# 1/rms rows through DRAM, a hand-ordered start and moved places in a hybrid decoder step

## The chip, the cores and the metric

The kernel runs on one core of one Trainium2 chip, as one launch. The metric is the device time of that launch in microseconds, the median of several runs. A profile of one execution is read beside it; it has its own time, which is named below.

The engines are called as in the profile: PE is the matrix engine (PEld its weight loads), DVE the vector engine, ACT the scalar engine, POOL the GpSimd engine, SP the engine that only issues DMAs here.

## The reference

One decoder layer. 2048 prompt tokens (zero initial state) and 8 decode rows (with given states) of width 1024 go through an RMS norm, one projection to eight groups of 512 columns, two chunkwise recurrences with four heads each, a norm by head, gates, an output projection, a residual and a final RMS norm. Cut to what matters:

```python
def mixer_layer(x, pos, s_ret, s_hg, norm_g, w_in, ret_g, hg_g, lb, w_out):
    h = rmsnorm(x, norm_g)
    p = (h @ w_in).astype(jnp.float32)
    rq, rk, rv, rg, hq, hf, hi, hgate = jnp.split(p, 8, axis=-1)
    rq = rotary(rq.reshape(B, L, RET_HEADS, RET_DK), pos)
    rk = rotary(rk.reshape(B, L, RET_HEADS, RET_DK), pos) * (RET_DK ** -0.5)
    ...
    o_ret, s_ret_new = chunked_decay_recurrence(rq, rk, rv, log_gamma, s_ret)
    o_ret = head_rmsnorm(o_ret, ret_g) * jax.nn.silu(rg)
    logf = jnp.logaddexp(jnp.log(lbf), jnp.log1p(-lbf) + jax.nn.log_sigmoid(hf))
    kin = (1.0 - lbf) * jax.nn.sigmoid(-hf)
    ...
    o_hg, s_hg_new = chunked_decay_recurrence(silu(hq), kin, hi, logf, s_hg)
    o_hg = head_rmsnorm(o_hg, hg_g) * jax.nn.silu(hgate)
    y = x + jnp.concatenate([o_ret, o_hg], axis=-1) @ w_out
```

Everything is fp32 in and out. The outputs are the two y, and the four new states.

## The kernel before

**Products.** Every large matrix product is done by Strassen's scheme on 2 x 2 blocks (seven products for eight, in the Winograd form, with block sums S1 to S4 of one side and T1 to T4 of the other), and each operand is split into a high and a low part of fp32r, so that a product of one 128-deep slice is three matmuls (high by high, high by low, low by high). One of the seven products is four slices, so 12 matmuls of 128 x 512. `product` (L872) issues half of one, 6 matmuls.

**Units and places.** The main loop has 38 units of seven products, numbered -6 to 31. A place is a number: unit u holds the places 7u to 7u + 7, and the seven products of a unit stand at 0, 1, 3, 4, 5, 6 and 9 behind 7u (`SLOTS`), so that one place is about one product. Units -6 to -1 make the values (columns rv and hi) of one pair of 128-token chunks each; 0 to 23 make the other six groups, three units for a head and half of the tokens (H: HGRN2 f and q, G: the gates, R: retention k and q); 24 to 31 are the output projection. All other work (splits, sums, gates, the recurrences, the decode rows, loads) is put on a list as `at(place, function)`, and at the end the list is emitted in order of place. `after(d, f)` puts f at d places behind the current one. The table `AT` holds most of the places.

**Queues.** Each engine works through its own instructions in the order in which they were emitted; this holds for PE in the whole kernel (`manual_schedule`), for DVE, ACT, POOL and SP from the second pair's ordered block on (`ORDERED`). Ahead of that block, in the start, the order of these four is left to the tile framework's own scheduler. A DMA on SP or POOL waits in its queue for its buffer or its source, and what is behind it waits too.

**The norm.** For each pair, `stats_load` and `stats_sum` (L332) square the token rows on ACT and `root` (L336, L228, L229) makes 1/rms on POOL: one value per partition (token), in `rs_all`. The transposed tokens (`x_t`) have the tokens along the free dimension, so 1/rms is needed as a row on all partitions. `spread_dg` (L356) makes a diagonal matrix of it on DVE, `spread` (L363) multiplies it on PE by a matrix of ones, and `tok_norm` (L372) on DVE multiplies tokens, gain `g_in` and this row from PSUM. `x1_dg` (L1316) and `x1_spread` (L701, L702) do the same for the second half of the tokens, and store two rows blocks to `rb_dram`, which `x1_rb` loads eight times later. `decode_dg` (L579) and `decode_spread` (L583, L585, L586) do it for the eight decode rows.

**The start.** After warm-up matmuls on constants (`wu`, L200, L203) pair 0 and then pair 1 are multiplied plainly, 96 matmuls each (`plain_k`, L465), while the W_v weights are loaded, split (`wv_split`, L233) and their differences T1 to T4 made (`wv_subs`, L514) and split (`wv_parts`, L233). Then the eight W_v slices are multiplied with the decode rows (`decode_values`, L556), for which `decode_inputs` (L532) multiplies them by the gain. Half of the differences of the slices 2 and 3 are made and split in the loop (`wv_late`).

**Blocks for later.** `blocks_sums` (L434) makes the differences T1 to T4 of the tokens of four pairs, half of them on POOL; POOL stores them (L430), SP loads them when they are needed (L1465).

**The recurrences.** `ret_rec` and `hgrn_rec` have steps with places of their own behind 7u (`AT["ret"]`, `AT["hgrn"]`): scores (s; s0 to s3, in which DVE updates k and q, L1188, L1191, and PE makes small score products, L1223, L1275, L1284), the value load, k transposed (k), the chunk updates (u), the states (st0, st1, DVE L1069), the outputs (o0, o1, L1076, L1078), and after scaling on ACT the transposition back and the gate (t0, t1, DVE L1103).

Of the kernel before, what the change touches and what calls it, by code (L numbers as in the profile page):

```python
# [15 lines left out]
ALU = mybir.AluOpType  # L16
# [32 lines left out]
def spooled(u):  # L49
# [10 lines left out]
          'load': 18.0,  # L60
# [10 lines left out]
 'ret': {'load': 12.0,  # L71
# [16 lines left out]
       'sS1': -1.4,  # L88
# [3 lines left out]
       'sA12': 1.4,  # L92
       'sS3': 2.4,
       'sA22': 3.05},
 're': {'A11': -3.4, 'S1': -2.4, 'S2': -1.4, 'S4': -0.4, 'A12': 0.6, 'S3': 1.6, 'A22': 2.6},
 'dec': {'mm': -1.97, 'mm0': -3.42, 'copy': -0.9, 'copy0': -2.4, 'sel': 0.7},
# [10 lines left out]
          'B22': (8.9, 8.95, 9.2, 9.75),  # L107
          'B21': (9.45, 9.85, 10.0, 10.3),
          'T3': (11.3, 11.3, 11.8, 11.8),
          'T4': (14.2, 14.2, 14.7, 14.7)},  # L110
# [4 lines left out]
           'lB21': 6.4,  # L115
           'lT3': 8.4,
           'lT4': 12.2,
           'B11': (3.0, 3.0, 3.5, 3.5),
# [3 lines left out]
           'B21': (9.45, 9.85, 10.0, 10.3),  # L122
# [6 lines left out]
 'wu': 17,  # L129
 'wop': (140.0, 1.8, 2.0, 2.6),  # L130
 'gate': {'G': 0.7, 'store': 1.2, 'R': 0.8, 'H': 0.7, 'root': 0.5, 'scale': 1.0, 'gt': 1.2, 'tr': 0.6},
 'fin': 0.75,
# [11 lines left out]
 'dhs': (-5.0, -2.2, -2.2, -1.5)}  # L144
# [5 lines left out]
def step_kernel(ctx, tc, a, out):  # L150
# [22 lines left out]
    vd_dram = dr.tile([2, NB, GW], F32, tag="vd_dram", name="vd_dram")  # L173
    v_dram = [
# [151 lines left out]
    def stats_sum(i, ahead=False):  # L326
# [23 lines left out]
    dgs = {}  # L350

    def spread_dg(i):
        dgs[i] = []
        for c in (2 * V_ORDER[i], 2 * V_ORDER[i] + 1):
            dg = vq.tile([P, P], F32, tag="dg", name=f"dg{c}", bufs=2)
            dve.tensor_scalar(dg, ident, rs_all[:, c : c + 1], None, op0=ALU.mult)  # L356
            dgs[i].append(dg)

    def spread(i):
        p = V_ORDER[i]  # L360
        pt = ps_tr.tile([P, 2, P], F32, tag="tr", name=f"prs{p}")
        for j, dg in enumerate(dgs[i]):
            pe.matmul(pt[:, j], ones, dg, start=True, stop=True)  # L363
        spread_to[i] = pt.rearrange("p a b -> p (a b)")
# [59 lines left out]
    def blocks_sums(i, n):  # L424
# [8 lines left out]
        def less(o, x, y):  # L433
            (dve if (i, n) in ((6, 0), (7, 1)) else pool).tensor_tensor(o, x, y, op=ALU.subtract)  # L434
# [35 lines left out]
    def tok_load0(i, k0, cuts=1):  # L470
        r = x0r[i, k0] = t_get([P, 2, 256], f"x0r{i}{k0}")
        for n in range(0, 2, 2 // cuts):
            kk = slice(n, n + 2 // cuts)
            sp.dma_start(r[:, kk], a["x_t"][V_ORDER[i], :, k0 + kk.start : k0 + kk.stop])
# [101 lines left out]
    dgd = vq.tile([NB, NB], F32, tag="dgd", name="dgd")  # L576

    def decode_dg():
        dve.tensor_scalar(dgd, ident[:NB, :NB], rsd[:, 1:2], None, op0=ALU.mult)  # L579

    def decode_spread():
        pt = ps_tr.tile([P, NB], F32, tag="tr", name="prsd")
        pe.matmul(pt, ones[:NB, :], dgd, start=True, stop=True)  # L583
        rb = vq.tile([P, NB], F32, tag="rbd", name="rbd")
        act.activation(rb, pt, AF.Copy)  # L585
        dve.tensor_tensor(  # L586
            xz[:, : 32 * KT].rearrange("p (k b) -> p k b", b=32)[:, :, :NB], xs,
            rb.unsqueeze(1).to_broadcast([P, KT, NB]), op=ALU.mult,
        )
# [11 lines left out]
    tok_load0(0, 0, 2)  # L601
    wv_load(0, 2)
    act.activation(lb[:, 0:1], zero, AF.Sigmoid)
    tok_load0(0, 4)
    wv_load(4, 2)
    for k in (0, 4):
        x_split0(0, k)
        wv_split(k)
    wv_load(1)
    wv_load(5)  # L610
    for k in (1, 5):
        x_split0(0, k)
        wv_split(k)
    tok_load0(0, 2)
# [12 lines left out]
    sp.dma_start(pk, a["pack"])  # L627
    stats(1)
    decode_inputs()
    for k in range(KT):  # L630
        x_split0(1, k)
    pv0 = {(c, ty): bank([P, GW], f"pv0{c}{ty}") for c in range(2) for ty in range(2)}
# [5 lines left out]
    for m, k in enumerate((0, 4, 1, 5, 2, 6, 3, 7)):  # L638
        decode_values(m, k)
    first, second = ("T1", "T2"), ("T3", "T4")  # L640
# [9 lines left out]
    with tc.manual_schedule(engines=ORDERED):  # L650
        stats_load(2)
        for c in range(2):
            for ty in range(2):
                plain_out(0, c, ty, pv0[c, ty])
        wv_subs(0, first + second)
        wv_parts(0, first + second)
        tok_load(2)
        ps = plain_next(0, 1)
        stats_sum(2, True)
        stats_load(3)  # L660
        wv_subs(1, first + second)
        wv_parts(1, first + second)
        tok_load(3)
        plain_out(1, 0, 1, ps)
        stats_sum(3, True)
        spread_dg(2)
        ps = plain_next(1, 1, lambda: spread(2))
# [3 lines left out]
        wv_subs(2, first[:1])  # L671
        wv_subs(3, first[:1])
# [4 lines left out]
        wv_parts(2, first[:1])  # L677
        wv_parts(3, first[:1])
        tok_norm(2, 1)
        tok_sums(2, 0)  # L680
        s_split(2, "S1")
        plain_out(1, 0, 0, ps)
        wv_subs(2, second[:1])
        wv_subs(3, second[:1])
        wv_subs(2, first[1:])
        wv_subs(3, first[1:])
        wv_parts(2, first[1:])
        wv_parts(3, first[1:])
        s_split(2, "S2")
        tok_sums(2, 1)  # L690
        s_split(2, "S4")
        ps = plain_next(1, 0)
# [5 lines left out]
    def blk_spread(blk, dg, dst):  # L698
        pt = ps_tr.tile([P, 4, P], F32, tag="tr", name=f"prb{blk}")
        for j in range(4):  # L700
            pe.matmul(pt[:, j], ones, dg[:, j], start=True, stop=True)  # L701
        act.activation(dst, pt.rearrange("p a b -> p (a b)"), AF.Copy)  # L702

# [1213 lines left out]
```

## Time and profile before

| | |
|---|---|
| median of 3 runs | 1004.38 us (1004.34 to 1006.59) |
| the profiled execution's own time | 1006.96 us |
| its span, first to last instruction | 1005.2 us |
| busy PE / DVE / ACT / POOL | 987.3 / 783.6 / 574.6 / 256.2 us |
| granted clock of PE, mean | 0.998 |
| moved by DMA | 244.56 MB, 243 GB/s |

How to read it: busy time is the time in which an engine had an instruction running; a wait row says which engine waited for whom, in total, how many times and the longest. The chain of waits is followed back from the last instruction, at each step to what released it. A fence shows rows as the profile has them; a line number is that of the kernel before. Between the last instruction and the execution's own time lie 1.8 us that the span doesn't hold.

### The profile page before, as it was taken

How to read it: one execution, taken by the hardware profiler on the slowest of the kernel's cores; microseconds unless marked ns; L12 is line 12 of the kernel's file. 1: busy time of each engine (PE TensorE's matmuls, PEld its weight loads, DVE VectorE, ACT ScalarE, POOL GpSimd, SP SyncE). 2: the span in 40 equal slices, each digit the busy share in tenths (PEclk: the TensorE clock that was granted, in tenths of full speed). 3: DMA queues.
4: the chain of work that ended last, by engine and by line, in shares of the span. 5: the costliest groups of instructions: out<-in, count | busy, mean ns of one | idle time of the engine just before them, and what ended most of it. 6: DMA issues, size and time to landing. Idle time of an engine off the chain costs nothing.

```text
span 1005.2 us, 22979 instructions
## 1 busy us (share of the span) xinstructions
PE 987.3 (98%) x8824; PEld 822.0 (82%) x8824; DVE 783.6 (78%) x1361; ACT 574.6 (57%) x1348; POOL 256.2 (25%) x404
## 2 busy tenths in 40 slices
PE   9999999999999999999999999999999999999997
PEld 8788877888888888888788788888888878877885
DVE  6797696879869978887898766877866799767774
ACT  7754523847655664765885555456467577524332
POOL 0211271112332433232012222222222602313121
PEclk9999999999999999999999999999999999999999
DMA  9746659838958878785985993993996396674522
GB/s 332 242 150 238 222 189 357 313 114 298 305 171 306 304 239 287 279 253 184 348 261 175 303 321 119 304 335 109 309 370 218 111 406 228 238 263 155 206 88 83
DMA packets 121340, 244.56 MB, mean 243 GB/s; under 512 B 12128, under 2 KB 52448, under 8 KB 118544
## 3 DMA queue, kind: packets, MB, share of 16 engines
q1 hardware_dynamic: 97968, 164.68, 48.9%
q0 software_dynamic: 22976, 78.17, 21.0%
q8 instruction: 69, 1.13, 0.5%
q14 instruction: 39, 0.32, 0.1%
q10 hardware_dynamic: 288, 0.27, 0.1%
HBM read 155.97 MB, written 90.24 MB: 245 GB/s over the span
## 4 chain that ended last, share of the span: by engine, by line
PE 84%; DVE 7%; ACT 4%; issue 2%; DMA 1%; POOL 1%; POOLq 0%; SPq 0%; DVEq 0%; ACTq 0%
PE aH L872 9%; PE aG L872 8%; PE aO L872 7%; PE aR L872 7%; PE aV L872 5%; PE eG L872 4%; PE eH L872 4%; PE pv L465 4%; PE eO L872 4%; PE eR L872 3%; PE eV L872 2%; PE bH L872 2%; PE bG L872 2%; PE bO L872 2%; PE bR L872 2%
## 5 line engine op out<-in xcount | busy, mean ns | idle before, releaser
L1639 ACT ACTIVATE yj<-xro 128x512 f32<-128x512 f32 x24 | 15.2, 632 | 66.9 <-DVE xro L716 33.2
L1202 ACT ACTIVATE qh<-kh 128x1024 f32<-128x1024 f32 x24 | 25.5, 1061 | 47.3 <-DVE kh L1188 47.3
L1188 DVE TENSOR_TENSOR kh<-kh,fph 128x512 f32<-128x512 f32 x48 | 32.9, 686 | 11.4 <-PE plh L1223 10.5
L949 ACT ACTIVATE sg<-g 128x512 f32<-128x512 f32 x26 | 16.4, 631 | 36.3 <-DVE g L716 35.8
L1082 ACT ACTIVATE obh<-poh 128x128 f32<-128x128 f32 x64 | 16.9, 287 | 32.5 <-PE poh L1078 32.5
L1191 DVE TENSOR_TENSOR qth<-qth,fph 128x512 f32<-128x512 f32 x48 | 32.9, 685 | 0.0
L1082 ACT ACTIVATE obr<-por 128x128 f32<-128x128 f32 x64 | 16.8, 276 | 27.3 <-PE por L1078 27.3
L716 DVE TENSOR_TENSOR xro<-aO,xro 128x512 f32<-128x512 f32 x33 | 22.5, 685 | 8.1 <-PE aO L872 7.8
L1106 POOL DMA_DIRECT2D o_dram<-gth x16 | 12.4, 773 | 62.6 <-DVE gth L1103 23.4
L1090 ACT ACTIVATE obh<-poh,orsh 128x128 f32<-128x128 f32 x64 | 18.2, 366 | 16.5 <-POOL orsh L229 16.4
L336 POOL TENSOR_TENSOR ms<-ms 128x2 f32<-128x2 f32 x8 | 3.0, 370 | 95.4 <-ACT xn L332 95.4
L956 POOL DMA_DIRECT2D g_dram<-g x31 | 16.9, 548 | 39.0 <-DVE g L952 33.9
L1090 ACT ACTIVATE obr<-por,orsr 128x128 f32<-128x128 f32 x64 | 18.2, 368 | 14.6 <-POOL orsr L229 14.6
L228 POOL TENSOR_SCALAR orsh<-omsh 128x4 f32<-128x4 f32 x16 | 4.9, 308 | 84.1 <-ACT obh L1082 83.8
L902 ACT ACTIVATE vo<-aV 128x512 f32<-128x512 f32 x12 | 7.1, 592 | 32.4 <-PE aV L872 32.1
L1069 DVE SCALAR_TENSOR_TENSOR sth<-sth,fph,puh 128x128 f32<-128x128 f32 x48 | 16.7, 347 | 11.0 <-PE poh L1078 8.5
L1106 POOL DMA_DIRECT2D o_dram<-gtr x16 | 12.5, 782 | 46.3 <-DVE g L716 14.0
L1076 PE MATMUL poh<-vh,A 128*128 128x128 f32 x128 | 24.0, 274 | 0.0
L1076 PE MATMUL por<-vr,A 128*128 128x128 f32 x128 | 24.0, 274 | 0.0
L228 POOL TENSOR_SCALAR orsr<-omsr,pk 128x4 f32<-128x4 f32 x16 | 7.6, 474 | 57.5 <-ACT obr L1082 57.5
L1653 DVE SCALAR_TENSOR_TENSOR xro<-xro,yms,fg 128x1024 f32<-128x1024 f32 (+1 forms) x16 | 19.9, 1245 | 3.0 <-POOL yms L1650 3.0
L1078 PE MATMUL poh<-sth,qth 128*128 128x128 f32 x112 | 21.7, 275 | 0.0
(1712 smaller groups left out, 3760.0 us busy)
## 6 DMA issues: line engine op xcount, KB each, us to landing
xn<-in_x_prompt SPq DMA_DIRECT2D x32, 256.0 KB, 4.7
v_dram<-vo SPq DMA_DIRECT2D x32, 256.0 KB, 3.4
xro<-in_x_prompt SPq DMA_DIRECT2D x16, 512.0 KB, 5.8
g_dram<-g POOLq DMA_DIRECT2D x31, 256.0 KB, 5.6
out_y_prompt<-xro POOLq DMA_DIRECT2D x15, 512.0 KB, 3.4
xr<-in_x_t SPq DMA_DIRECT2D x12, 512.0 KB, 5.7
vh<-v_dram SPq DMA_DIRECT2D x16, 256.0 KB, 8.0
gth<-g_dram SPq DMA_DIRECT2D x16, 256.0 KB, 6.8
```

Of the source, the lines that this page charges most:

```text
L465: pe.matmul(ps, xx, ww, start=(first and n == 0), stop=(last and n == 2))
L716: dve.tensor_tensor(o, x, y, op=ALU.add)
L872: pe.matmul(ps, w[i], x[j], start=(first and k == 0 and m == 0), stop=(k == 3 and m == 2), skip_group_check=True,)
L1076: pe.matmul(po[:, j], s_ctx["A"][:, c], box["v"][g][:, j], start=True, stop=src is None)
L1078: pe.matmul(po[:, j], qcol(c), src, start=False, stop=True)
L1082: act.activation(ob[:, j], po[:, j], AF.Square, accum_out=ms[:, j : j + 1])
L1090: act.activation(ob[:, j], po[:, j], AF.Copy, scale=rs[:, j : j + 1])
L1106: after(AT["gate"]["tr"], lambda: pool.dma_start(o_dram[c0 : c0 + 4, ty, :, h].rearrange("c p t -> p c t"), gt.rearrange("p (c t) -> p c t ...
L1188: dve.tensor_tensor(kv[:, :, 0, :], kv[:, :, 0, :], two[:, :, 1:2].to_broadcast([P, nb, b]), op=ALU.mult)
L1191: dve.tensor_tensor(qv[:, :, 1, :], qv[:, :, 1, :], two[:, :, 0:1].to_broadcast([P, nb, b]), op=ALU.mult)
L1202: act.activation(kept_k, k, AF.Copy)
L1653: dve.scalar_tensor_tensor(x[:, cc], x[:, cc], ms[:, 0:1], fg[:, cc], op0=ALU.mult, op1=ALU.mult)
```

## The change

- The 1/rms values of each pair are stored by POOL to `rs_dram` as soon as they are made (256 values of 4 bytes), and `spread` is now a DMA on SP that reads two rows of 128 and repeats them on all partitions. `spread_dg`, `x1_dg`, `x1_spread` and their matmuls go; `x1_rb` reads four rows of `rs_dram`. The decode rows go the same way through `rsd_dram`, with the store and the load in unit -5 and the product in unit -3 as before.
- In the start the loads of the first tokens are cut finer, the decode rows' columns of the packed constants are loaded early, the first four decode products stand inside pair 0's products, and all W_v differences and parts stand ahead of the loop. The ordered block of pair 1 is arranged anew; `wu` has 18 small warm-up matmuls more.
- In `blocks_sums` all differences are made on DVE.
- Some 30 places change by 0.05 to 1.5. Units above 20 have tables of their own (`retL`, `hgrnL`), which for the most part hold the old places; `hd` moves s2 and s3 of unit 3 by -0.5; `w24` and `vp` hold places, of which `half` (4.7 to 4.2) and the last of `s` (9.6 to 9.1) are new.

```diff
- 'ret': {'load': 12.0,
+ 'ret': {'load': 12.5,
...
-         'o0': 15.5,
+         'o0': 15.0,
          'st1': 15.7,
          'o1': 17.1,
-         'last': 17.6,
-         't0': 19.01,
-         't1': 21.7},
+         'last': 17.1,
+         't0': 19.51,
+         't1': 23.2},
...
- 'dec': {'mm': -1.97, 'mm0': -3.42, 'copy': -0.9, 'copy0': -2.4, 'sel': 0.7},
+ 'dec': {'mm': -1.97, 'mm0': -3.92, 'copy': -0.9, 'copy0': -2.4, 'sel': 0.7},
...
-           'B21': (9.45, 9.85, 10.0, 10.3),
+           'B21': (9.45, 9.85, 10.25, 10.55),
...
- 'wu': 17,
+ 'wu': 35,
...
- 'fin': 0.75,
+ 'fin': 1.0,
...
             rsqrt_mean(rs_all[:, 2 * p : 2 * p + 2], ms[:, 0:2], D, EPS)
+            pool.dma_start(rs_dram[2 * p : 2 * p + 2].rearrange("c p -> p c"), rs_all[:, 2 * p : 2 * p + 2])
...
-    def spread_dg(i):
-        dgs[i] = []
-        for c in (2 * V_ORDER[i], 2 * V_ORDER[i] + 1):
-            dg = vq.tile([P, P], F32, tag="dg", name=f"dg{c}", bufs=2)
-            dve.tensor_scalar(dg, ident, rs_all[:, c : c + 1], None, op0=ALU.mult)
-            dgs[i].append(dg)
-
     def spread(i):
         p = V_ORDER[i]
-        pt = ps_tr.tile([P, 2, P], F32, tag="tr", name=f"prs{p}")
-        for j, dg in enumerate(dgs[i]):
-            pe.matmul(pt[:, j], ones, dg, start=True, stop=True)
-        spread_to[i] = pt.rearrange("p a b -> p (a b)")
+        spread_to[i] = vq.tile([P, 2 * P], F32, tag="rsb", name=f"rsb{p}", bufs=2)
+        sp.dma_start(spread_to[i].rearrange("p (c t) -> p c t", c=2), rs_dram[2 * p : 2 * p + 2].partition_broadcast(P))
...
         def less(o, x, y):
-            (dve if (i, n) in ((6, 0), (7, 1)) else pool).tensor_tensor(o, x, y, op=ALU.subtract)
+            dve.tensor_tensor(o, x, y, op=ALU.subtract)
...
+        if kk == 1:
+            decode_inputs()
+            for m, k in enumerate((0, 4, 1, 5)):
+                decode_values(m, k)
+            for k in range(2):
+                wv_subs(k, first + second)
+                wv_parts(k, first + second)
+    for m, k in enumerate((2, 6, 3, 7)):
+        decode_values(m + 4, k)
...
         stats_load(2)
+        stats_sum(2, True)
         for c in range(2):
             for ty in range(2):
                 plain_out(0, c, ty, pv0[c, ty])
-        wv_subs(0, first + second)
-        wv_parts(0, first + second)
+        for k in (2, 3):
+            wv_subs(k, first + second)
         tok_load(2)
         ps = plain_next(0, 1)
-        stats_sum(2, True)
+        spread(2)
         stats_load(3)
-        wv_subs(1, first + second)
-        wv_parts(1, first + second)
         tok_load(3)
+        for op in first + second:
+            for k in (2, 3):
+                wv_parts(k, (op,))
...
     def x1_rb(n, k):
         xd["rb"] = t_get([P, GW], f"rb{n}{k}")
-        sp.dma_start(xd["rb"], rb_dram[n])
+        c = 8 + 4 * TB[n]
+        sp.dma_start(xd["rb"].rearrange("p (c t) -> p c t", c=4), rs_dram[c : c + 4].partition_broadcast(P))
```

More of the change, by code (lines that the diff above doesn't have):

```diff
@@ L468, in step_kernel, with tok_load0 @@
     x0_left = {(i, k): [0, 1] for i in range(2) for k in range(4)}
[L470 to L474, printed above, removed]
+    def tok_load0(i, k0, ks=(0, 1)):
+        if (i, k0) not in x0r:
+            x0r[i, k0] = t_get([P, 2, 256], f"x0r{i}{k0}")
+        kk = slice(ks[0], ks[-1] + 1)
+        sp.dma_start(x0r[i, k0][:, kk], a["x_t"][V_ORDER[i], :, k0 + kk.start : k0 + kk.stop])
     def x_split0(i, k):
@@ L626, in step_kernel @@
         tok_load0(1, k)
-    sp.dma_start(pk, a["pack"])
+    for x in (slice(0, xs_at.start), slice(xs_at.stop, PACK_W)):
+        sp.dma_start(pk[:, x], a["pack"][:, x])
     stats(1)
-    decode_inputs()
     for k in range(KT):
         x_split0(1, k)
+    first, second = ("T1", "T2"), ("T3", "T4")
     pv0 = {(c, ty): bank([P, GW], f"pv0{c}{ty}") for c in range(2) for ty in range(2)}
@@ L697, in step_kernel @@
     dve.tensor_copy(lmask, packed("lmask"))
[L698 to L702, printed above, removed]
     def raw(b):
@@ L1769, in step_kernel @@
     at(7 * 12 + 4.1, lambda: tables(1))
-    for n in range(2):
-        at(9.2 + n, lambda n=n: x1_dg(n))
-        at(10.6 + n, lambda n=n: x1_spread(n))
     for k in range(4):
```

161 lines of the change are left out of this document (86 added, 75 removed).

## The prediction

> **What bounds the kernel now.** I read the page first, then who TensorE (PE) waited for, then the busy time of single stretches, then the chain of waits where PE does what the change takes away.
>
> ```profile
> span 1005.2 us, 22979 instructions
> PE 987.3 (98%) x8824; PEld 822.0 (82%) x8824; DVE 783.6 (78%) x1361; ACT 574.6 (57%) x1348; POOL 256.2 (25%) x404
> PE 84%; DVE 7%; ACT 4%; issue 2%; DMA 1%; POOL 1%; POOLq 0%; SPq 0%; DVEq 0%; ACTq 0%
> ```
>
> PE is busy in 987.3 of 1005.2 us and makes 84% of the chain. A busy PE need not be PE at its peak, so I check its pace in a fence below: twelve products take 2.73 us, 227 ns each, and the waits are short and few:
>
> ```profile
> PE plh L1284 <- DVE qth L1191: 2.2, 2, 1.5
> PE plh L1223 <- issue: 2.0, 2, 1.0
> PE aO L872 <- DVE xro L716: 0.9, 1, 0.9
> PE par L1140 <- DVE qr L716: 0.7, 1, 0.7
> PE poth L1101 <- DVE gth L1103: 0.6, 1, 0.6
> PE plh L1223 <- DVE qth L1191: 0.5, 2, 0.3
> PE aV L872 <- DVE vo L716: 0.4, 1, 0.4
> PE eH L872 <- DVE x1T1l L713: 0.4, 1, 0.4
> PE prs L363 <- DVE dg L356: 0.2, 1, 0.2
> ```
>
> After the first microseconds every wait on an engine names VectorE (DVE): 2.2 + 0.9 + 0.7 + 0.6 + 0.5 + 0.4 + 0.4 + 0.2 = 5.9 us. So a change can win here in two ways: less work on PE, nearly one for one, and DVE work that PE waits for moved earlier. It can lose where DVE, full in two stretches of the start, is given more (columns: time, then busy PE, PE loads, DVE, ScalarE (ACT), GpSimd (POOL), granted clock, DMA share, GB/s):
>
> ```profile
> 50.00:75.00 25.00, 25.00 (x114) 20.76 (x113) 23.12 (x41) 14.77 (x32) 2.98 (x7) 1.00 0.45 148
> 125.00:150.00 25.00, 25.00 (x111) 20.03 (x110) 23.18 (x31) 7.38 (x13) 19.39 (x19) 1.00 0.55 182
> 975.00:1006.00 31.00, 22.92 (x102) 18.64 (x100) 15.88 (x22) 8.23 (x19) 5.57 (x14) 0.93 0.18 71
> ```
>
> **The change part by part. 1: matmuls that leave PE.** The 1/rms rows were spread over the partitions by PE; now DMAs do it. The matmuls that go, with their time on PE:
>
> ```profile
> 57.77 2.73 PE eV L872 x12
> 60.50 0.44 PE prs L363 x4
> 205.86 0.89 PE prb L701 x8
> 209.50 0.89 PE prb L701 x8
> ```
>
> ```profile
> L363 PE MATMUL prs<-dg,ones x24: 272/275/348, 40.7 to 136.9; 128*128 128x128 f32 x24
> L583 PE MATMUL prsd<-dgd,ones x2: 251/262/272, 127.6 to 127.8; 8*128 8x8 f32 x2
> ```
>
> The 24 instructions of prs are six groups of four, 6 x 0.44 = 2.64 us; prb 2 x 0.89 = 1.78 us; prsd, two instructions of 0.26 us that overlap, 0.3 us. Together 4.7 us. All stand in PE's own order between products, so they shorten the path unless PE then stands and waits. With them go 12 DVE products (dg), two larger ones (dgx), three ACT evictions, and the wait of prs for dg (0.2 us).
>
> **2: the DMAs instead.** Each pair of chunks gets a POOL store of 256 single fp32 values, behind the root on POOL's queue, and an SP broadcast, half a place ahead of the products with g_in that use it (tok_norm, L372). No such store is in the trace. The rows for bounds:
>
> ```profile
> 65.24 0.69 POOL L229 TENSOR_TENSOR rs_all<-rs_all,mhalf 128x2 f32<-128x2 f32 x1
> 79.09 1.65 DVE L372 SCALAR_TENSOR_TENSOR xr<-xr,g_in,prs 128x256 f32<-128x256 f32 x4
> x_dram<-bT POOLq DMA_DIRECT2D x8, 256.0 KB, 2.8
> vh<-v_dram SPq DMA_DIRECT2D x16, 256.0 KB, 8.0
> ```
>
> From the end of the root (65.93) to the use (79.09) there are 13.2 us. At the quickest row the round trip is 2 x 2.8 = 5.6 us, at the slowest 2 x 8.0 = 16.0 us: between 7.6 us to spare and 2.8 us late. I take the short end, nearer in size (1 KB stored, 128 KB spread), so it costs nothing; what hides it is the rest of the previous pair's products. Behind the waiting broadcast on SP stand the next pair's x loads; they are due a whole pair later. The reads of the 1/rms rows for the second half of the tokens (x1_rb) change their source alone: nothing. The decode row makes the same trip with 14 places between load and use: nothing.
>
> **3: first two pairs.** All W_v differences and their high and low parts are finished before the loop instead of partly in it: no work saved, but six DVE instructions of W_v (0.69 us each, by the row of part 4) and the late halves of pair 2 leave the stretch 50 to 75, where DVE has 23.12 of 25 us. The decode rows of the first four k now stand inside pair 0's products, and 18 more small warm-up matmuls before it:
>
> ```profile
> 5.99 0.41 PE wu L203 x34
> ```
>
> 17 of them (34 instructions) take 0.41 us, so 18 cost 0.43 us at most; the lower bound is 0, if the first product's data is later anyway. I take 0.4.
>
> **4: block differences from POOL to DVE (blocks_sums).** Eight of sixteen move. The rows, of POOL, of DVE, and of two DVE instructions of one shape, beside POOL and alone:
>
> ```profile
> L434 POOL TENSOR_TENSOR bs70B<-bs70B,bs70B x1: 1745/1745/1745, 145.3 to 145.3; 128x512 f32<-128x512 f32 x1
> L434 DVE TENSOR_TENSOR bs60B<-bs60B,bs60B x1: 685/685/685, 128.1 to 128.1; 128x512 f32<-128x512 f32 x1
> 136.48 2.32 DVE L233 TENSOR_TENSOR x0B21l<-xr,x0B21h 128x1024 fp32r<-128x1024 f32 x1
> L233 DVE TENSOR_TENSOR x0B21l<-xr,x0B21h 128x1024 fp32r<-128x1024 f32 x1 | 1.2, 1218 | 0.0
> ```
>
> DVE takes on 8 x 0.69 = 5.5 us in a stretch where it has 1.8 us free, which alone would stop PE. But beside a POOL difference the same DVE instruction takes 2.32 us instead of 1.22: each costs DVE up to 1.1 us already, 8 x 1.1 = 8.8 us at most, 0 at least. So DVE's load there changes by between +5.5 and -3.3 us; I take 0, and the wait for vo at the end of that stretch (0.4 us) as gone, since the differences no longer queue behind one another at 1.75 us and the block loads come sooner.
>
> **5: moved places.** The second low part of the last B21 goes from 10.3 to 10.55, which is behind the last rotation of unit 23 (at 10.31). The chain of waits has just this order ahead of the 0.7 us wait of par:
>
> ```profile
> 837.01 1.14 DVE woB21l L713
> 838.15 0.60 DVE qr L967
> 839.39 0.69 DVE qr L716
> ```
>
> 1.14 us leave the path of a 0.7 us wait: gone. Likewise t1 of the retention tail moves from 21.7 to 23.2, behind the update that the HGRN2 scores wait for:
>
> ```profile
> 799.28 0.60 DVE gtr L1103
> 801.75 0.61 DVE kh L1188
> ```
>
> 0.60 us are taken from ahead of both waits of plh at L1223 (0.5 us in all): gone. The output step o0 comes half a product sooner on PE, the decode products (mm0) of each third unit too, and two score steps of unit 3: each arrives up to 2.73/2 = 1.36 us earlier at data that is as late as before. 0 to 1.4 us each; I take 0.35 for all. Gates a quarter place later (fin), weight splits later, loads half a place along SP's queue: due places later, and the 8.0 us of the slowest load bounds them; nothing, and 1 us if that cover goes.
>
> **Sum**, on the profiled execution, 1005.2 span of 1006.96 us: -4.7 (matmuls) - 0.2 (prs) - 0.4 (vo) - 0.7 (par) - 0.5 (plh) + 0.4 (warm-up) + 0.35 = -5.75, so 1001.2 us. That execution lies 2.6 us above the median shown, 1004.38; from the median the same sum gives **998.6 us**.
>
> **Rivals.** (B) DVE gets so much air that its other waits go as well: 2.2 + 0.9 + 0.6 + 0.4 = 4.1 us more, 994.5. For it: every wait names DVE. Against it: L1284 (2.2) and xro (0.9) have no edit right ahead of them.
>
> (C) The waits only move on: 1004.38 - 4.7 + 0.75 = 1000.4.
>
> (D) DVE becomes the bound of the first 150 us: the differences arrive late, or the broadcast is late by the 2.8 us above in the two full stretches. Five broadcasts in the loop, two of them there: 5.6 us back, 1004.2, no change. Against it: at the quickest row there are 7.6 us to spare, and the six instructions that leave the first full stretch.
>
> (E) Slower. PE stands at the first decode rows, because the product with g_in that they need keeps its place among DVE's splits of pair 1:
>
> ```profile
> 17.59 0.39 PE L465 MATMUL pv<-wvT1h,x0B11h 128*128 128x512 f32 x1
> 21.14 0.69 DVE L233 TENSOR_TENSOR wvT1l<-wvr,wvT1h 128x512 fp32r<-128x512 f32 x1 [3.90 <-ACT wvT1h L232]
> 25.62 0.22 DVE L532 TENSOR_TENSOR pk<-pk,g_in 128x64 f32<-128x64 f32 x1
> 27.02 0.19 DVE L697 CAST lmask<-pk 128x80 uint8<-128x80 f32 x1
> ```
>
> PE would ask at about 17.6 and get it at 25.84: 8.2 us, so 998.6 + 8.2 = 1006.8. It decides from 5.8 us of waiting on. The 16 differences and parts of k 0 and 1 queue behind those rows on DVE, 16 x 0.69 = 11 us, and where they come late as well it is over 1007.4. Against it: the columns needed now load early, DVE is idle for 3.90 us before 21.14, and L697, far later in the code, ran at 27.02, so the order outside the hand-ordered part follows what is ready. [...]
>
> (F) The change does not do what it says: PE isn't the bound, and the matmuls that go only filled waits: 1004.4. [...] Against it: the even 227 ns and clock 1.00.
>
> **How the numbers follow.** Forecast 0.58, B 0.13, C 0.12, D 0.09, E 0.05, F 0.03. Under 0.3% (3 us) a change can't be told from none, so faster means below 1001.4: forecast, B and nearly all of C, 0.80. Same is D, F, the low half of E and the rest of C, 0.16; slower, above 1007.4, most of E with its 11 us, 0.04. The range leaves out a little of B below and D, E, F above: 994.0 to 1002.0.
>
> **What would show it.** Right: no prs, prb, prsd on PE; the loop's first product (aV) begins 0.2 us or so sooner; par and L1223 no longer in PE's waits; DVE near L233 at 136 us back at 1.2 us; the normalising L372 not waiting for a DMA. Wrong: a wait of PE for pk or for DVE before 30 us; rows of PE waiting for DVE in 50 to 150 us that sum to over 3 us; new rows for poh or pdp.

## The result, and the profile after

The change makes the kernel slower: 1040.14 us (median, 1036.25 to 1042.84) against 1004.94 us (1004.26 to 1007.16) beside it, a ratio of 1.034 (95% interval 1.032 to 1.037), so some 35 us are lost where 5.75 were to be won. The profiled execution took 1036.25 us. The page after, its span and busy times:

```profile
span 1034.5 us, 22962 instructions
PE 993.6 (96%) x8818; PEld 824.0 (80%) x8818; DVE 779.9 (75%) x1354; ACT 576.5 (56%) x1345; POOL 252.3 (24%) x403
```

PE's busy time has not fallen with the matmuls that left, from 987.3 to 993.6 us: an instruction counts longer while the clock is halved (behind the 13.0 us wait shown below, at a granted clock of 0.50, the products' matmuls take 0.63 us, at full clock 0.39). Its waits after (engine, line and tile that waited, for whom: us in total, times, longest):

```profile
PE aV L902 <- ACT vo L622: 13.0, 1, 13.0
PE aV L902 <- DVE vo L744: 7.7, 3, 3.7
PE plh L1253 <- issue: 6.3, 2, 4.2
PE eV L902 <- DVE s2S L309: 3.1, 1, 3.1
```

The waits of the loop that the prediction named for DVE (par, and plh for qth at L1223) are gone from this list. In their place stand 23.8 us of waits of the value products aV and eV, which only the first 200 us have, and, at the line that was L1223 (now L1253), 6.3 us without a releaser where 2.0 stood. The stretches of the start after (columns as in the prediction):

```profile
50.00:75.00 25.00, 11.99 (x47) 9.49 (x47) 9.15 (x16) 8.50 (x18) 2.35 (x4) 0.73 0.70 178
75.00:100.00 25.00, 21.94 (x91) 17.70 (x90) 13.41 (x24) 11.05 (x25) 3.95 (x9) 0.93 0.53 166
125.00:150.00 25.00, 21.31 (x88) 17.23 (x87) 17.71 (x33) 11.27 (x22) 5.49 (x10) 0.93 0.88 218
150.00:175.00 25.00, 20.99 (x84) 16.60 (x84) 17.48 (x31) 6.59 (x10) 5.83 (x8) 0.93 0.83 207
```

PE is idle for half of 50 to 75 us, and DVE, which was full there (23.12), is now idle for two thirds: both wait. The clock is below 1 in each of the four (0.73, and 0.93 three times): PE's four longest waits in these stretches (13.0, 3.7, 3.4 and 3.1 us) are each followed by matmuls 427 ns apart in place of 227, at a granted clock of 0.50. In unit starts, read from PE's records: unit -6 begins at 68.7 us (before 54.9), unit 0 at 204.2 (before 175.6), and PE's last instruction ends 29.5 us later. So nearly all that this execution loses is lost before unit 0; it is the quickest of the six, 3.9 us below their median, and where the others lose the rest is not shown.

What the start waits for: the store of 1/rms by its line, then who waited for the rows on DVE, then SP's own waits in the first 200 us.

```profile
L375 POOL DMA_DIRECT2D rs_dram<-rs_all x8: 776/790/958, 24.6 to 148.2; - x8
...
DMA to landing us min/median/max: 7.6/10.7/13.3
```

```profile
L399 DVE SCALAR_TENSOR_TENSOR xr<-xr,g_in,rsb 128x256 f32<-128x256 f32 x48 | 19.8, 478 | 32.0 <-DMA rsb<-rs_dram 30.9 <-issue 1.1
```

```profile
SPq L391 <- DMA rs_dram<-rs_all: 18.8, 2, 11.7
```

A store of 1 KB lands after 10.7 us, longer than any of the 256 KB transfers whose rows the prediction showed. DVE stands 30.9 us for the rows, and SP, behind whose broadcast the next loads queue, 18.8. And the store is not alone late: transfers of the first 200 us (KB each, median us from issue to landing), of the kernel before and of the one after:

```profile
v_dram<-vo SPq DMA_DIRECT2D x32, 256.0 KB, 3.4
x_dram<-bT POOLq DMA_DIRECT2D x8, 256.0 KB, 2.8
b_dram<-xr POOLq DMA_DIRECT2D x2, 512.0 KB, 3.8
```

```profile
v_dram<-vo SPq DMA_DIRECT2D x29, 256.0 KB, 7.9
x_dram<-bT POOLq DMA_DIRECT2D x8, 256.0 KB, 5.8
b_dram<-xr POOLq DMA_DIRECT2D x2, 512.0 KB, 11.2
...
rsb<-rs_dram SPq DMA_DIRECT2D x6, 128.0 KB, 5.6
```

The first three stores are the same in both kernels, and they land two to three times as late. The last row is the new broadcast.

### The profile page after: what moved, and what is told of

It is laid out like the page before. It is cut to its first block, busy times and chain, and to the rows that moved or that the text cites. A ratio compares the mean times of both kernels' runs of the same rounds, so it can differ in the third digit from the quotient of the medians.

```text
span 1034.5 us, 22962 instructions
## 1 busy us (share of the span) xinstructions
PE 993.6 (96%) x8818; PEld 824.0 (80%) x8818; DVE 779.9 (75%) x1354; ACT 576.5 (56%) x1345; POOL 252.3 (24%) x403
## 4 chain that ended last, share of the span: by engine, by line
PE 76%; DVE 3%; DMA 2%; ACT 2%; issue 2%; POOL 0%; POOLq 0%; SPq 0%; DVEq 0%; ACTq 0%
PE aG L902 8%; PE aR L902 8%; PE aO L902 8%; PE aH L902 8%; PE eR L902 5%; PE eG L902 4%; PE eO L902 4%; PE eH L902 4%; PE bG L902 2%; PE bR L902 2%; PE bH L902 2%; PE plh L1253 2%; PE bO L902 2%; PE puh L1083 1%; PE pdp L806 1%
## 5 line engine op out<-in xcount | busy, mean ns | idle before, releaser
L1650 ACT ACTIVATE yj<-xro 128x512 f32<-128x512 f32 x29 | 18.3, 633 | 74.1 <-DVE xro L744 40.4
L399 DVE SCALAR_TENSOR_TENSOR xr<-xr,g_in,rsb 128x256 f32<-128x256 f32 x48 | 19.8, 478 | 32.0 <-DMA rsb<-rs_dram 30.9
L369 ACT ACTIVATE xn<-xn 128x512 f32<-128x512 f32 x32 | 19.9, 624 | 15.3 <-DMA xn<-in_x_prompt 13.5
L902 PE MATMUL aV<-wvT1h,x0B11h 128*128 128x512 f32 x24 | 11.1, 463 | 17.9 <-ACT vo L622 13.0
L1099 DVE SCALAR_TENSOR_TENSOR sth<-sth,fph,puh 128x128 f32<-128x128 f32 x48 | 16.7, 347 | 10.4 <-PE poh L1108 7.5
L1108 PE MATMUL por<-str,qr 128*128 128x128 f32 x112 | 21.8, 276 | 0.4 <-DVE str L1097 0.4
```

The source lines that it names most:

```text
L369: act.activation(r, r, AF.Square, accum_out=ms[:, 2 * h + j : 2 * h + j + 1])
L902: pe.matmul(ps, w[i], x[j], start=(first and k == 0 and m == 0), stop=(k == 3 and m == 2), skip_group_check=True,)
L1108: pe.matmul(po[:, j], qcol(c), src, start=False, stop=True)
```

## The experiments

Every ratio is to the kernel before, run beside the variant, with its 95% interval. Two theories stood at first. R: the loss is the latency of the rows' round trip, which DVE waits for. W: it lies elsewhere in the change. All of the first four variants keep stores of 1/rms in pieces of a few bytes.

**1. The pairs' rows by PE again, the stores kept** (in the kernel after):

```diff
     def spread(i):
         p = V_ORDER[i]
-        sp.dma_start(spread_to[i].rearrange(...), rs_dram[2 * p : 2 * p + 2].partition_broadcast(P))
+        for j, dg in enumerate(dgs[i]):
+            pe.matmul(pt[:, j], ones, dg, start=True, stop=True)
```

> The changed kernel, with the 1/rms rows of pairs 2 to 7 spread by PE again (diagonal matrix on DVE, matmul by ones); all else of the change stays, the stores to rs_dram too. Theory R (the round trip through DRAM: the store of 256 single values lands 7.6 to 13.3 us after its issue, SP stands behind it, DVE waits 30.9 us in five waits for the rows): nearly all of the 28.6 us that are lost before unit 0 come back; 1003 to 1008 us, no wait of PE over 2 us before unit 0. Theory W (the start arranged anew and the differences on DVE make DVE and ACT late, and the late rows only show it): 1030 us or more, PE still waits about 13 us at the first product of the loop.

Measured: 1034.9 us, 1.029 (1.025 to 1.033). R falls as the whole cause: nothing waits for the rows in the first 200 us any more, and most of the loss is still there. It does not fall altogether, because the variant has a wait of its own, PE for the scaled unit matrix dg, which DVE makes late:

```profile
PE prs L401 <- DVE dg L394: 10.2, 2, 5.7
```

W's time came, but not its sign: at the first product of the loop PE waits 3.6 us, not 13. The transfers of that stretch are as late as before:

```profile
v_dram<-vo SPq DMA_DIRECT2D x30, 256.0 KB, 7.7
b_dram<-xr POOLq DMA_DIRECT2D x2, 512.0 KB, 11.4
```

**2. The route alone, in the kernel before** (stores and broadcasts for the pairs, all else old):

```diff
+            pool.dma_start(rs_dram[2 * p : 2 * p + 2].rearrange("c p -> p c"), rs_all[:, 2 * p : 2 * p + 2])
...
-        spread_dg(2)
-        ps = plain_next(1, 1, lambda: spread(2))
+        spread(2)
+        ps = plain_next(1, 1)
```

> The kernel before, with one part of the change alone: the 1/rms rows of pairs 2 to 7 stored by POOL and broadcast by SP (12 small matmuls and their diagonals go); the rows of the second half and the decode rows stay on PE, no place is moved. Theory R: slower by 20 to 32 us, 1025 to 1037, with PE waits at the first products of units -6 to -1. Theory W: 1002 to 1005.

Measured: 1055.0 us, 1.049 (1.046 to 1.051), more than the whole change. So the rest of the change softens the loss and doesn't make all of it; the time lies above what R had expected. PE's longest waits are of the kind seen above:

```profile
PE aV L863 <- DVE vo L707: 16.0, 3, 9.9
PE aV L863 <- ACT vo L585: 13.7, 1, 13.7
```

**3. Half as many pieces, twice as large** (in the kernel after: rows of two values, 8 bytes; DVE reads the row with a stride):

```diff
-            pool.dma_start(rs_dram[2 * p : 2 * p + 2].rearrange("c p -> p c"), rs_all[:, 2 * p : 2 * p + 2])
+            pool.dma_start(rs_dram[p], rs_all[:, 2 * p : 2 * p + 2])
```

> The changed kernel, with the two values of a partition stored side by side: 128 pieces of 8 bytes instead of 256 of 4; the broadcast stays one contiguous row, DVE reads it with a stride of two. If the store's time goes with its number of pieces, it lands in 4 to 7 us instead of 7.6 to 13.3, and about half of the loss goes: 1015 to 1025 us. If it is a fixed price of any such store, nothing changes: 1036 to 1043.

Measured: 1014.61 us, 1.008 (1.006 to 1.011). Three quarters of the loss go, a little more than expected. The store lands sooner, and so do its neighbours (two views, the store's line and the transfers of the first 200 us):

```profile
DMA to landing us min/median/max: 3.1/3.9/6.9
```

```profile
v_dram<-vo SPq DMA_DIRECT2D x32, 256.0 KB, 4.1
```

**4. The same 4-byte store from ACT's queue** (`act.dma_start` in place of `pool.dma_start`, in the kernel after):

> The changed kernel, with the same store of 256 single values issued by ACT on its hardware queue instead of by POOL (in the loop 0.7 of a place after the root). If the price is that of POOL's software queue, the store lands in 3 to 5 us and the loss falls to under 10 us: under 1015. If it is that of the many pieces, it lands in 7 to 13 us as before: 1034 to 1045.

Measured: 1035.35 us, 1.030 (1.028 to 1.032); the store's line:

```profile
DMA to landing us min/median/max: 6.6/9.0/10.1
```

So the issuing queue is not the cause. In this variant the records hold the pieces themselves: the 256 of a store begin within 0.2 to 1.0 us (2.3 for the last store) and take 9 ns each, yet the store lands some 9 us later. Meanwhile packets of other stores hang: of GpSimd's 4 KB packets, which took at most 0.44 us in the first 200 us of the kernel before, some take up to 6.6 us here, and up to 5.6 in the kernel after. That gave the next theory, S: the small writes hold up the writes to DRAM behind them.

**5. The stores alone** (in the kernel before; nothing reads them):

```diff
             rsqrt_mean(rs_all[:, 2 * p : 2 * p + 2], ms[:, 0:2], D, EPS)
+            pool.dma_start(rs_dram[2 * p : 2 * p + 2].rearrange("c p -> p c"), rs_all[:, 2 * p : 2 * p + 2])
```

> The kernel before with the eight stores of 1/rms added and nothing that reads them: 256 pieces of 4 bytes into 1 KB of DRAM each, on the GpSimd queue, while TensorE goes on spreading the rows. Theory S (the stores hold up the DRAM writes behind them: in the changed kernel single packets of 4 KB took up to 5.6 us, before at most 0.44): the time rises by most of what the variant with TensorE's spreading rose by, to 1020 to 1036, and the W_v products' stores land in over 6 us in the first 200 us against 3.4. Rival (what costs is the rest of the change, its order and its places): no more than 1008.

Measured: 1032.22 us against 1006.46, 1.025 (1.023 to 1.026). Eight stores of 1 KB that nobody waits for cost 25.8 us. The store's line, then its neighbours:

```profile
DMA to landing us min/median/max: 8.6/10.4/13.5
```

```profile
v_dram<-vo SPq DMA_DIRECT2D x29, 256.0 KB, 6.2
xr<-in_x_t SPq DMA_DIRECT2D x12, 512.0 KB, 11.4
b_dram<-xr POOLq DMA_DIRECT2D x2, 512.0 KB, 11.1
```

The middle row is a load, and before it took 5.7 us: not writes alone are late. How the lateness reaches PE is seen in the chain of work that ends at a late product (start, duration) and in PE's waits: a store that takes 11.9 us, a load of tokens that SP issues when it has landed and that takes 10.7, and then the engines that work on them.

```profile
34.43 11.92 DMA v_dram<-vo
...
46.74 10.67 DMA xn<-in_x_prompt
```

```profile
PE prs L365 <- DVE dg L358: 9.1, 3, 7.0
PE aV L874 <- ACT vo L596: 8.7, 1, 8.7
```

Experiment 2 has the same stores and readers for them, and no matmuls of prs: it loses 49.3 us where this loses 25.8. So in the old order of the start, waiting for the rows costs some 23.5 us on top, nearly as much as the stores themselves.

**6 and 7. The same stores with the pieces apart.** The tile gets a last dimension of 128 values (512 bytes) or of 16 (64 bytes), of which the first is written:

```diff
-    rs_dram = dr.tile([T // P, P], F32, tag="rs_dram", name="rs_dram")
+    rs_dram = dr.tile([T // P, P, 16], F32, tag="rs_dram", name="rs_dram")
```

> The same eight stores without a reader, the same 256 pieces of 4 bytes, but each piece goes to a place of its own 512 bytes from the next (64 KB a column). If the price goes by the number of pieces, the time is that of the stores into 1 KB, 1020 to 1036. If it comes from many small writes into the same few lines of DRAM, the stores land in under 5 us and the time is within 5 us of the kernel before, 1003 to 1010.

> The kernel before with the eight unread stores, 256 pieces of 4 bytes, 64 bytes from one another. If what counts is that several pieces fall into one stretch of 64 bytes, the time is that of the kernel before, 1004 to 1008. If the stretch is 512 bytes, eight pieces still fall into each and the time lies between the 1006 of pieces 512 bytes apart and the 1032 of pieces side by side: 1010 to 1025.

Measured, 512 bytes apart: 1006.36 us, 1.000 (0.999 to 1.001). 64 bytes apart: 1006.68 us, 1.000 (0.999 to 1.001). The store's line and its neighbour, first at 512, then at 64 bytes:

```profile
DMA to landing us min/median/max: 2.0/2.6/6.0
```

```profile
v_dram<-vo SPq DMA_DIRECT2D x32, 256.0 KB, 3.0
```

```profile
DMA to landing us min/median/max: 2.0/2.6/5.7
```

```profile
v_dram<-vo SPq DMA_DIRECT2D x32, 256.0 KB, 3.1
```

The number of pieces, their size and their queue are those of experiment 5; only the place of the pieces differs, and the whole cost is gone. The records show each of these stores as 16 packets of 64 bytes, and these take no longer side by side (median 38 ns) than 64 bytes apart (39 ns): what differs comes after them. So it is not that the pieces are small and many, but where they fall: here 4-byte pieces cost 25.8 us when they lie side by side, and nothing (1.000) at 64 bytes from one another. Side by side is not all of it, though. The 8-byte pieces of experiment 3 do so too, eight to each 64 bytes, and landed in 3.9 us; a store of only eight words side by side, for the decode rows, landed in 3.0 us in the kernel after. No run has a distance between 4 and 64 bytes, or tells the stretch of 64 bytes from the 1 KB in which all the pieces lie (16 KB at 64 bytes apart).

**8. The rest of the change** (the kernel after with the tokens' rows by PE as before and no store of them; start, decode rows, DVE's differences and places stay):

> The changed kernel with the token rows of 1/rms made as before (TensorE spreads the pairs' rows and the rows of the blocks kept raw; no store of 1/rms at all); the ramp's new order, the decode rows through DRAM, the sums on VectorE and the moved places stay. Theory S: all of the loss goes, and the rest is worth what the forecast's other terms give, -0.2 -0.4 -0.7 -0.5 +0.4 +0.35 = -1.05 us: about 1004, within 1000 to 1006. Rival (the rest costs): 1015 or more.

Measured: 1023.75 us, 1.016 (1.014 to 1.018), above S's forecast and within its rival's. It loses 6.3 us before unit -6, at one wait:

```profile
PE prs L399 <- DVE dg L392: 4.3, 1, 4.3
```

The unit matrix is scaled behind the W_v parts that the new order puts ahead of it. This wait belongs to the variant, for the kernel after has no dg. The rest comes later, in waits without a releaser. So I tried the parts.

**9. The moved places alone** (in the kernel before, from unit 0 on):

> The kernel before with only the moved places between products from unit 0 on (recurrences, second-half tables from unit 21, weights, decode, swaps, output product). By the forecast's terms -0.7 -0.5 +0.35 it is 0 to 2 us faster, 1003 to 1005; if the places collide it is 2 to 10 us slower, with new waits of TensorE after unit 0.

Measured: 1011.92 us, 1.005 (1.003 to 1.007), with a spread of single runs (1005.05 to 1019.54) much wider than that of the kernel before. In its profile the waits of par and of plh at the old L1223 for DVE are gone, as forecast, and that of poth too. One of 0.9 us for the decode weights is new, and that of plh at the old L1284 has grown from 2.2 us to 2.7.

**10 and 11. The places in two halves:** the recurrences' tables alone, and all others alone.

> The kernel before with only the recurrences' moved places (the two recurrence tables, their second forms from unit 21, the scores shifted by 0.5 in unit 3). All moved places together cost 5.5 us. If the recurrences carry it, for they issue the many small matmuls before which TensorE stood longer, this is 1009 or more; if weights, decode and swaps carry it, it is 1004 to 1007.

> The kernel before with only the other moved places (weights, decode, swaps of both kinds, the output product). If these carry the 5.5 us, for the decode products of the first unit of three are now half a place earlier and wait for their weights, this is 1009 or more; if the recurrences carry it, 1004 to 1007.

Measured: 1006.86 us, 1.001 (1.000 to 1.002), and 1007.0 us, 1.002 (1.001 to 1.003). Neither half carries the 5.5 us; they do not add. In the first half par still waits 0.3 us and plh at the old L1223 1.1 us for DVE; in the second both waits are gone, and the one at the old L1284 is 3.3 us.

**12. The differences of the blocks on DVE alone** (in the kernel before, the change's line in `blocks_sums`):

> The kernel before with only the differences of the blocks of the last two pairs all on VectorE (8 of 16 were on GpSimd). The forecast had this at no change: 1004 to 1007. If VectorE is late by it for the products of the first units, 1008 or more.

Measured: 1006.74 us, 1.000 (0.999 to 1.001): no change. PE's wait for vo, which the prediction took as gone, is 0.5 us (before 0.4).

**13. Experiment 8 with the scaling earlier:**

```diff
         tok_load(3)
+        spread_dg(2)
         for op in first + second:
...
         stats_sum(3, True)
-        spread_dg(2)
```

> The changed kernel with rows spread by TensorE as before, and VectorE scaling the third pair's unit matrix ahead of the parts of W_v instead of behind them. TensorE stood 4.3 us there and then ran 1.8 us at half clock, which was the whole of the 6.3 us lost before the first unit: without it the time falls from 1023.75 by about 6 us to 1015 to 1019. If the ramp is late for another reason, it stays above 1021.

Measured: 1016.96 us, 1.010 (1.008 to 1.012), as expected. Unit 0 now begins at 175.2 us, before 175.6; still 10.8 us are missing, behind it. PE's waits:

```profile
PE plh L1268 <- issue: 4.1, 1, 4.1
...
PE potr L1146 <- issue: 2.5, 1, 2.5
PE aG L917 <- issue: 2.0, 2, 1.8
```

**14. The longer warm-up alone** (in the kernel before):

```diff
- 'wu': 17,
+ 'wu': 35,
```

> The kernel before with only the longer warm-up (35 small matmuls in place of 17). By the forecast 0.4 us; the first product starts 1.3 us later in the changed kernel. If the place in TensorE's instruction stream sets the waits without a releaser, they change by several us in sum, either way, against the 3.5 us of the kernel before, and the time with them; if not, they stay within 1 us and the time is 1006 to 1008.

Measured: 1015.31 us against 1006.13, 1.008 (1.007 to 1.010). Eighteen tiny matmuls in the first 8 us (36 in the records, with their weight loads 72 instructions) cost 9.2 us. By unit starts 2.7 us are lost at unit 0 and 9.0 at unit 24, most of it in steps: 2.5 us in unit 5, 4.2 around the start of unit 14. PE's waits, and its timeline at these two steps (start, duration; in brackets the idle time before):

```profile
PE plh L1223 <- issue: 2.6, 2, 2.3
PE aG L872 <- issue: 2.6, 1, 2.6
...
PE bG L872 <- issue: 0.8, 1, 0.8
```

```profile
318.18 0.52 PE L1223 MATMUL plh<-qth,kh 128*32 128x16 f32 x41
321.04 0.37 PE L1223 MATMUL plh<-qth,kh 128*32 128x16 f32 x21 [2.35 <-issue]
```

```profile
548.92 0.39 PE L872 MATMUL aG<-x1T3h,w13S 128*128 128x512 f32 x1
551.88 0.39 PE L872 MATMUL aG<-x1T3l,w13S 128*128 128x512 f32 x1 [2.57 <-issue]
```

PE stops in the middle of a run of like matmuls, and the profile shows nothing that it waits for. Of the 8.6 us by which PE ends later in this profile, such waits make 3.0 (6.5 in all, before 3.5), and two stretches of 3.4 us at half clock, which the kernel before doesn't have (from 546 to 556 us, at the second step, the mean granted clock is 0.83, before 1.00), 3.4 by my estimate (half of both).

**15. Experiment 13 with the old warm-up:**

> The variant with the early scaling and rows spread by TensorE, with the old, shorter warm-up. If the place in the instruction stream sets the waits, the 8.6 us of waits without a releaser shrink and the time falls by more than 3 us from 1016.96; if not, it stays within 2 us, less the 1.3 us by which the first product starts earlier.

Measured: 1006.26 us against 1006.13, 1.000 (0.999 to 1.002): 10.7 us less than with the long one. PE's waits without a releaser:

```profile
PE plh L1268 <- issue: 2.2, 1, 2.2
...
PE pah L1268 <- issue: 1.2, 1, 1.2
```

3.4 us in place of 8.6 in the rows shown. So the other parts of the change together, with the tokens' rows still made by PE and with neither their 4-byte stores nor the longer warm-up, come out even.

**16 and 17. The route with whole rows** (in the kernel after): PE turns the columns of 1/rms into rows, one transpose for the four raw pairs and one for each later pair, and rows of 512 bytes are stored; the broadcasts stand 1.4 to 1.8 places earlier than in the kernel after, and the third pair is spread by PE. Once with the new places, once with the old ones.

```diff
+    def rows(c, n):
+        pt = ps_tr.tile([P, P], F32, tag="tr", name=f"prr{c}")
+        pe.transpose(pt[:n], rs_all[:, c : c + n], ident)
+        rt = vq.tile([8, P], F32, tag="rt", name=f"rt{c}", bufs=2)
+        act.activation(rt[:n], pt[:n], AF.Copy)
+        pool.dma_start(rs_dram[c : c + n], rt[:n])
```

> The changed kernel with the route through DRAM kept and only the shape of its store changed: TensorE turns the columns of 1/rms into rows (one transpose for the four raw pairs, one for each later pair), ScalarE copies them, and rows of 512 bytes are stored (2 or 8 pieces); the third pair, which has no time for the round trip in the ramp, is spread by TensorE as before. If the many small writes are the loss, it is gone: -3.8 us for the spreading matmuls (2.2 of 2.64, 1.78 and 0.3, less some 0.5 for the transposes) and +5.5 for the moved places give about 1008, within 1003 to 1012. If the route itself is too long for the places it is given, VectorE waits for the rows in the first 150 us and it is 1015 or more.

> The same with the places of the kernel before from unit 0 on. If effects add, 5.5 us less than with the moved places: about 1002, within 999 to 1006, faster than both kernels. If the moved places fit the new ramp better than the old, it is no faster than the one with moved places.

Measured: 1008.91 us, 1.003 (1.002 to 1.005), and 1012.06 us, 1.006 (1.005 to 1.008). With whole rows stored (and the broadcasts earlier, and one pair kept on PE) the change falls from 1.034 to 1.003, so the route itself is not too long at these places. That the old places do worse here contradicts "effects add"; the profile of this one has a wait of 3.7 us without a releaser at plh, that of the other 1.3 there. In the first of the two, PE stands at its own transposes:

```profile
PE prr L394 <- DVE xr L421: 2.0, 1, 2.0
PE prr L394 <- POOL rs_all L266: 1.9, 3, 1.0
```

**18. Whole rows, with less of these waits** (the first transpose in a bank of its own, the others half a place later):

```diff
-        at(U + 4.8, lambda i=i: rows(2 * V_ORDER[i + 2], 2))
+        at(U + 5.3, lambda i=i: rows(2 * V_ORDER[i + 2], 2))
```

> The variant with whole rows, with the first transpose in a bank of its own (it waited 2.0 us for VectorE to read the third pair's rows out of the bank) and the later ones half a place later (they waited 1.9 us for the roots). If these waits and the halved clock behind the longer one are what it lacked, it is 4 to 5 us faster than the 1008.9 with them: about 1004, within 1002 to 1006. If the delays only move to the transfer of the rows, it stays at 1008 or more.

Measured: 1005.02 us against 1006.13, 0.998 (0.997 to 1.000): the quickest of all, by about 1 us, hardly more than can be told. Of the waits at the transposes 1.0 us is left. The store's line of this variant, in which 2 or 8 rows are written at once:

```profile
DMA to landing us min/median/max: 1.6/1.7/2.5
```

The same with the old warm-up was not tried.

## Why the prediction was wrong

The forecast was 998.6 us with 994.0 to 1002.0, and slower at 0.04; it is 1040.14. Two terms failed, and no rival had either at anything like its size.

**Part 2, "it costs nothing".** This is the step that made most of the error, in three ways. How the loss in the kernel after divides between the second and the third is not shown; stores whose pieces fall otherwise take away most of both (experiment 3, and 16 to 18 with one pair left on PE).

- *The price.* The short end, 2.8 us, was taken because it was "nearer in size". The store lands in 10.7 us, and with 5.6 for the broadcast the trip takes 16.3, just over the long end of 16.0. That end was no bound either: 8.0 us was called the slowest row, but the same profile has 9.1 (dS<-in_state_ret, 256 KB). The row nearest in size was not the nearest in kind: no store in the trace is made of pieces of 4 bytes.
- *The margin.* The 13.2 us between root and use are those of the loop. For the third pair, in the start, the records of before have the root end at 38.5 us and PE spread the row at 40.7; there the trip has no cover: DVE stands 12.1 us for these rows, and PE waits 13.0 us at the loop's first product. Rival D had the mechanism (the broadcast late, DVE standing), but only in two stretches and at 2.8 us each.
- *The neighbours.* The prediction asked what the new DMAs wait for and not what waits for them below the queues. With no reader at all the stores cost 25.8 us in the kernel before (experiment 5): the stores shown beside them land at 6 to 11 us instead of 3 to 4, and behind those the buffers, the loads and PE are late. Placed 64 bytes apart they cost nothing (experiment 7).

**Part 3, the warm-up, "I take 0.4".** The bounds were 0 and 0.43, from the time that the matmuls take themselves. In the kernel before it costs 9.2 us (experiment 14), and taken out of experiment 13 it gives 10.7 back. Both are shown. It is no fixed price: experiment 18 has the longer warm-up too, is no slower than the kernel before, and has 3.4 us of waits without a releaser, about as many as before. Why is in part argued: PE's waits without a releaser change in place and length when 72 instructions are put ahead of the stream, and each of the longer ones stands by a packet of the instruction queue, whose row in the kernel before (packets, MB, share) is

```profile
q8 instruction: 69, 1.13, 0.5%
```

that is 16 KB each, 64 bytes for each of PE's 17648 recorded instructions; with the 72 more of experiment 14 there are 70 packets. In all 20 traces, each of the 47 waits of PE without a releaser that last 0.5 us or more ends 2.2 to 3.1 us after such a packet begins (the five of the kernels before and after 2.3 to 2.8 us), where a moment taken at random has one there in about 6 of 100 cases (69 packets, 0.9 us behind each, in 1005 us). So these waits go with the packets of instructions. Why they come at few of the 69 packets no run shows. My reading is that the warm-up moves the places in PE's stream at which it needs the next packet to moments at which that packet has not come. The prediction saw 3.5 us of such waits (2.0 and, not quoted there, 1.5 of pah) and no term of its sum let them change.

**Part 1, the matmuls.** They are gone, and where nothing else stood in the way they paid: in experiment 18, PE begins unit 2 at 215.1 us against 218.1 before, though its start has the longer warm-up. Of these 3.0 us 1.8 come between the starts of units 1 and 2, where the 1.78 us of prb went; the kernel after gains as much there (28.6 us late at unit 1, 26.8 at unit 2). This is the variant nearest to the forecast's sum, and it ends 1 us ahead of the kernel before, not 5.75. The other matmuls of the 4.7 us were not measured by themselves.

**Part 4** was right in time, 0 foreseen and no change measured; its 0.4 us for the wait for vo did not come (0.5 us in experiment 12). **Part 3's new order** was right in that DVE has air in the start and PE does not wait for the decode rows: rival E did not come. Of **part 5** the mechanism was right in part and the gain not: with all the places moved the waits of par and L1223 went, 1.2 us in all, but 0.5 of that came back at L1284 (2.2 to 2.7 us), as rival C has it, and the time rose by 1.0 and 1.2 us in the halves and 5.5 together. How much of this is once more the place in the instruction stream, and how much the wait for decode weights half a place earlier (0.9 us, within the 1.4 allowed), stays open.

**The sum of the loss.** The stores (25.8) and the warm-up (9.2), each alone in the kernel before, make 35.0 us of the 35.2 between the medians of 1040.14 and 1004.94, and without these two experiment 15 is level. That the sum fits is luck as far as the runs show. In the new order the stores without readers in the start cost about 12 us, or 14 with the matmuls of prb that only one of the two has, not 25.8 (experiment 1 loses 29.2 us, experiment 8 17.3); the rows are waited for too, and PE's matmuls are gone. The warm-up alone loses 6 us behind unit 0, but the kernel after, in its profile, only 0.9.

**What it would show.** Of the signs set down ahead, prs, prb and prsd are gone, and par too; L1223 no longer waits for DVE, but longer without a releaser; the low part of B21 on DVE is back at 1.22 us; "the loop's first product 0.2 us sooner" came 13.8 us later, and "L372 not waiting for a DMA" turned into 30.9 us of just that. The sign for wrong, over 3 us of PE waiting for DVE in 50 to 150 us, appeared.

## What to carry to other kernels

Before a small result goes through DRAM, look at where its pieces fall: the values here sat one to a partition and were written as single words, and words side by side, 256 to a store, had some other transfers land 2 to 3 times as late (in the kernel after, the stores of vo after 7.9 us instead of 3.4), while the same words 64 bytes apart (1.000), or rows turned on TensorE first (0.998 to 1.006), cost next to nothing. Price a new DMA by a row of the same shape of pieces, at the place with the least slack, and ask what it does to the transfers already there. This kernel, which keeps TensorE full, also proved sensitive to how many instructions stand ahead (72 more cost it 9.2 us in experiment 14), so measure each edit that adds instructions alone, however cheap.

## What was not expected of the hardware

- 256 writes of 4 bytes side by side into 1 KB land after 10.4 us (median), 64 or 512 bytes apart after 2.6, and 128 writes of 8 bytes into 1 KB after 3.9. In the kernel with the first kind other stores of the first 200 us land in 6 to 11 us instead of 3 to 4, and single 4 KB packets take up to 6.6 us instead of 0.44 at most.
- Issued by GpSimd or by ScalarE, the price is about the same, 10.7 or 9.0 us.
- Eighteen tiny matmuls at the start (0.4 us of work) cost the kernel before 9.2 us, in steps of 1 to 4 us hundreds of microseconds later; in experiment 18 they stand too, and nothing is lost.
- Each of 47 waits of TensorE of 0.5 us or more that the profile can't explain ends 2.2 to 3.1 us after a 16 KB packet of the instruction queue begins.
